# Scaling two projections inside PSUM, and three subtractions per weight tile instead of four, in a hybrid encoder layer

## The chip, the cores and the metric

The kernel runs on one core of one Trainium2 chip. Times are device microseconds of one execution. The core has five engines that run side by side and meet at semaphores: TensorE (PE, matrix products; PEld are its weight loads), VectorE (DVE), ScalarE (ACT), GpSimd (POOL) and SyncE (SP, which here only issues DMAs). Operands lie in SBUF, matrix products land in banks of PSUM. GpSimd works on SBUF tiles alone in this kernel.

## What is computed

One layer of an encoder trunk on 512 tokens of width 1024, in fp32. Cut to what matters here:

```python
h = rmsnorm(x, pre_mix_norm)
z, xbc, dt_raw, q, k, v, gates = split_cols(h @ w_in, IN_SPLITS)
y_ssd = ssd_branch(z, xbc, dt_raw, ...)          # bidirectional scan, 8 groups of 4 heads
y_attn = window_attention(q, k, v, sink, rel_table) @ w_attn_out   # 16 query heads, 4 key heads, width 64
g_ssd, g_attn = split(sigmoid(gates + b_gate))
x = x + rmsnorm((g_ssd * y_ssd + g_attn * y_attn) @ w_o, post_mix_norm)
f = square(relu(rmsnorm(x, pre_mlp_norm) @ w_mlp_in)) @ w_mlp_out
x = x + rmsnorm(f, post_mlp_norm)
```

The change touches the projections that give k (256 columns) and the first part of q, and the preparation of most weight tiles.

## The kernel before, in words

**Products in three parts.** An fp32 product is made of three fast ones. A factor is split into a high part, its rounding to a shorter format (a copy on ScalarE), and a low part, factor minus high part (a subtraction on VectorE or GpSimd). `mm3` (its matmuls are all recorded on the helper line L454) then adds high times high, high times low and low times high into one PSUM bank.

**Weight tiles.** A weight tile is 128 x 1024: eight blocks of 128 columns, one block for each step of a sum over 1024. SP loads it into one of three `wr` buffers. `chunk_split` makes `wh` with one ScalarE copy (L529) and `wl` with GpSimd subtractions (L533): `eng` is `"pppp"`, so four subtractions of 256 columns. Three tiles have 768 columns, so four pieces of 192, and one tile of 768 columns comes with three letters, so three pieces of 256. `wh` and `wl` have three buffers each. The weights of `w_o` and `w_mlp_out` are prepared elsewhere (L1621, L1624), and so are the tiles of the first products (L631, L633).

**Quanta.** The program is a list of quanta. One quantum of `cm` takes one weight tile, runs 24 matmuls (eight blocks, three each, 512 columns) into one bank of the tag `pp`, and calls `done(ps)`, which empties the bank. There are three `pp` banks, taken in turn, and five `ps` banks for everything else. The first quanta are three for v and dt (into `ps`), two for k, two for q with the tokens not yet normalised ("raw"), and then x, q, x, q, B and so on, with the normalised tokens `h`. Between k's first and second quantum the bank `rb` is taken, in which the reciprocal norm of each token is spread over all partitions; ScalarE copies it into the SBUF tile `self.rb` (L738), and eight VectorE operations read the bank to make the normalised tokens (L742).

**After a k quantum** (`k_done`), VectorE multiplies the bank by `self.rb` into the SBUF tile `kf` (L867). From then on the bank is free. Four tiles come of each two heads: for either half of the partitions (a head of width 64) a tile `KH` that holds the head's high part in both halves, and a tile `KL` that holds its low part in both halves. The first is a ScalarE copy from `kf` (L872), the low part a VectorE subtraction from `kf` (L873), and two further copies (L874, L875) bring them to the other half.

**After a raw q quantum** (`done` in `q_quantum`), VectorE scales the bank by 0.125 and by `self.rb` into the SBUF tile `qf` (L898); ScalarE copies a head's high part out of `qf`, blocks of tokens in reverse order (L906), and VectorE subtracts for the low part (L907). The later q quanta do the same straight out of the bank (L911, L912).

**Order.** Every instruction is emitted in program order and then ordered anew by `Planner`: for each engine it plays the program through with costs that are written in the code, gives each instruction a due time that follows from the matmul that needs it, and fixes the order found as each engine's queue. TensorE keeps nearly the program's order. Instructions that use the same PSUM bank are all ordered one after another, whatever they do; instructions that touch the same SBUF columns are ordered if one of them writes. The costs hold a lock between VectorE and GpSimd for some operations. So any edit can move instructions anywhere in the program.

**Slots.** Other SBUF tiles come from 83 slots, handed out in the order in which they were freed; `kf` and `qf` take a slot each for a while.

Of the kernel before, what the change touches and what calls it, by code (L numbers as in the profile page):

```python
# [10 lines left out]
F32 = mybir.dt.float32  # L11
F32R = mybir.dt.float32r
AF = mybir.ActivationFunctionType
ALU = mybir.AluOpType
# [30 lines left out]
FAR, AHEAD = (2,3,5,6,8,9,11,12,), 5  # L45

BACK = 3
WARM = 8
V_CHUNKS = ((0, 2), (2, 5), (5, 8))
W_CHUNKS = ((0, 1), (1, 2), (2, 5), (5, 8))  # L50
# [50 lines left out]
class Slots:  # L101
# [5 lines left out]
    def get(self, name, shape=(128, 512), dtype=F32):  # L107
        s = self.free.popleft()
        self.n += 1
        t = self.pool.tile(list(shape), dtype, tag=f"s{s}", name=f"{name}_{self.n}", bufs=1)  # L110
        self.tags[t.tensor.name] = f"s{s}", 1
        self.slot[id(t)] = (s, t)
        return t
# [279 lines left out]
class Trunk:  # L393
# [117 lines left out]
    def chunk_split(self, i):  # L511
        if len(self.chunks[i]) == 3:
            self.parts[i] = self.chunks[i][1]()
            return
        _, kk, n, eng = self.chunks[i]
        raw = self.raw.pop(i)
        m = kk * n
        hi = self.wp.tile([128, 1024], F32R, tag="wh", name=self.name("wh"), bufs=SPL)
        self.tags[hi.tensor.name] = "wh", SPL
        if eng == "both":  # L520
            view = hi[:, :2 * m].rearrange("p (k u n) -> p k u n", k=kk, u=2)
            r3 = raw.rearrange("p (k n) -> p k n", k=kk)
            self.nc.scalar.copy(view[:, :, 0], r3)
            self.nc.gpsimd.tensor_tensor(view[:, :, 1], r3, view[:, :, 0].bitcast(F32), op=ALU.subtract)
            self.parts[i] = view.rearrange("p k u n -> p k (u n)")
            return
        lo = self.wp.tile([128, 1024], F32R, tag="wl", name=self.name("wl"), bufs=SPL)
        self.tags[lo.tensor.name] = "wl", SPL
        self.nc.scalar.copy(hi[:, :m], raw)  # L529
        engines = {"v": self.nc.vector, "p": self.nc.gpsimd}  # L530
        for e, c in zip(eng, range(0, m, m // len(eng))):
            c = slice(c, c + m // len(eng))
            engines[e].tensor_tensor(lo[:, c], raw[:, c], hi[:, c].bitcast(F32), op=ALU.subtract)  # L533
        v = lambda t: t[:, :m].rearrange("p (k n) -> p k n", k=kk)
        self.parts[i] = (v(hi), v(lo))

# [127 lines left out]
    def start(self):  # L664
# [13 lines left out]
        pg = self.bank("pp")  # L678
        for _ in range(WARM):
            self.mm(pg[:, :128], ones, ones, True, True)  # L680
# [179 lines left out]
    def kv_quanta(self):  # L860
        nc = self.nc
        get = self.slots.get
        self.KH, self.KL = [], []

        def k_done(ps):
            x = get("kf")
            nc.vector.tensor_tensor(x, ps, self.rb, op=ALU.mult)  # L867
            for j in range(2):
                a = slice(j * 64, j * 64 + 64)
                b = slice(64 - j * 64, 128 - j * 64)  # L870
                KH, KL = get("KH", dtype=F32R), get("KL", dtype=F32R)
                nc.scalar.copy(KH[a], x[a])  # L872
                nc.vector.tensor_tensor(KL[a], x[a], KH[a].bitcast(F32), op=ALU.subtract)  # L873
                nc.scalar.copy(KH[b], x[a])  # L874
                nc.scalar.copy(KL[b], KL[a])  # L875
                self.KH.append(KH)
                self.KL.append(KL)
            self.slots.put(x)

        hh = lambda: self.hr  # L880
        return [self.cm(self.d_w_in_b, C_K - 64 + 128 * i, hh, k_done) for i in range(2)]
# [5 lines left out]
    def q_quantum(self, i):  # L887

        nc = self.nc

        blocks = lambda ap: ap.rearrange("p (n t) -> p n t", t=128)

        raw = i < RAW_Q

        def done(ps):
            if raw:
                x = self.slots.get("qf")
                nc.vector.scalar_tensor_tensor(x, ps, 0.125, self.rb, op0=ALU.mult, op1=ALU.mult)  # L898
            for u in range(2):
                a = slice(u * 64, u * 64 + 64)  # L900
                b = slice(64 - u * 64, 128 - u * 64)
                q = self.slots.get("Q", dtype=F32R)
                if raw:
                    self.Q[2 * i + u] = q
                    back = self.backward(x[a])
                    nc.scalar.copy(blocks(q[a]), back)  # L906
                    nc.vector.tensor_tensor(blocks(q[b]), back, blocks(q[a]).bitcast(F32), op=ALU.subtract)  # L907
                    continue
                self.Q[2 * i + u] = q
                back = self.backward(ps[a])  # L910
                nc.scalar.activation(blocks(q[a]), back, AF.Copy, scale=0.125)  # L911
                nc.vector.scalar_tensor_tensor(blocks(q[b]), back, 0.125, blocks(q[a]).bitcast(F32), op0=ALU.mult, op1=ALU.subtract)  # L912

            if raw:
                self.slots.put(x)
            if i == RAW_Q - 1:
                self.slots.put(self.rb, *sum(self.hr, ()))

        return self.cm(self.d_w_in_b, C_Q - 64 + 128 * i, lambda: self.hr if raw else self.h, done)

    def attn_bias(self, h):
# [643 lines left out]
    def folded_quanta(self, part):  # L1565
# [95 lines left out]
        if last:  # L1661
            if part == 3:
                self.at(len(self.quanta) + BACK, self.load_x1)
            for name, lead in MIX_LEAD if part == "o" else (('B11', 4), ('B22', 4), ('B12', 4), ('B21', 3)):
# [122 lines left out]
```

## Time and profile before

| | us |
|---|---|
| median of 3 runs | 1072.91 |
| lowest, highest | 1072.71, 1074.02 |
| the profiled execution | 1075.79 |
| span of its profile, first to last instruction | 1074.0 |
| TensorE busy in the span | 1060.2 (99%) |
| GpSimd busy | 796.0 (74%) |
| VectorE busy | 771.8 (72%) |
| ScalarE busy | 658.4 (61%) |
| mean granted TensorE clock | 0.998 of full speed |

The profiled execution took 2.88 us more than the median and 1.8 us more than its own span. A row of a group names line, engine, operation, what it writes and reads, its shape and count, then busy time and mean duration, then the idle time of the engine before such instructions and what ended it. A row of the timeline has its start and length in us, and in brackets the idle time before it. Neighbouring instructions of one engine overlap a little in the record, and the ends of matmuls are modelled, so the step from start to start says more on TensorE than the length.

### The profile page before, as it was taken

To read this page: it belongs to the slowest core of one execution; us is meant where nothing else is said; L and a number is where in the kernel's file an instruction comes from. 1 tells how busy PE (TensorE), PEld (TensorE's weight loads), DVE (VectorE), ACT (ScalarE), POOL (GpSimd) and SP (SyncE) were. 2 spreads that over 40 slices of the span, in tenths; PEclk is the share of its full clock that TensorE was granted. 3 is DMA by queue.
4 is the path that set the end of the run, shared out by engine and by line. 5 is a ranking of instruction groups with operands and counts; after the bars stand their busy time and mean duration, and the time that the engine had idled before them with its cause. 6 is when DMAs were issued, how large, how long until landed. Compare 5 with 4: busy or idle time off the path is not lost.

```text
span 1074.0 us, 16639 instructions
## 1 busy us (share of the span) xinstructions
PE 1060.2 (99%) x5542; PEld 893.8 (83%) x5542; DVE 771.8 (72%) x1354; ACT 658.4 (61%) x1409; POOL 796.0 (74%) x991
## 2 busy tenths in 40 slices
PE   9999999999999999999999999999999999999997
PEld 8878888888888888888888788889888888888885
DVE  6986877797795868787877626698663574574588
ACT  7875786676686857676777424466555444444552
POOL 4856557557668798999989956215587898898994
PEclk9999999999999999999999999999999999999999
DMA  8443333433434535255535444317221421434232
GB/s 316 140 128 101 102 102 111 130 102 116 123 99 128 163 102 171 88 142 148 170 92 157 159 147 148 111 59 263 89 69 65 153 98 60 157 96 141 78 99 78
DMA packets 62085, 134.25 MB, mean 125 GB/s; under 512 B 9128, under 2 KB 18984, under 8 KB 62000
## 3 DMA queue, kind: packets, MB, share of 16 engines
q1 hardware_dynamic: 61712, 132.96, 38.4%
q8 instruction: 43, 0.70, 0.3%
q14 instruction: 42, 0.34, 0.1%
q10 hardware_dynamic: 288, 0.23, 0.1%
HBM read 128.68 MB, written 4.49 MB: 124 GB/s over the span
## 4 chain that ended last, share of the span: by engine, by line
PE 86%; DVE 7%; POOL 2%; issue 2%; DMA 2%; ACT 1%; DVEq 0%; SPq 0%; POOLq 0%; ACTq 0%
PE pp L454 54%; PE ps L454 30%; PE ps L458 2%; DMA x<-in_x 1%; POOL wl L533 1%; DVE yl L1321 1%; POOL w L1222 1%; DVE P L941 1%; DVE u L1017 1%; DVE xt L742 0%; DVE P L955 0%; DMA xt<-in_xt 0%; DVE h L745 0%; DVE dtw L816 0%; DVE u L1024 0%
## 5 line engine op out<-in xcount | busy, mean ns | idle before, releaser
L533 POOL TENSOR_TENSOR wl<-wr,wh 128x256 fp32r<-128x256 f32 (+1 forms) x519 | 415.4, 830 | 180.7 <-ACT wh L529 172.7
L454 PE MATMUL pp<-h,wh 128*128 128x512 f32 (+1 forms) x1664 | 504.6, 385 | 0.0
L454 PEld LDWEIGHTS pp<-h,wh 128*128 128x128 f32 x1664 | 306.3, 188 | 59.2 <-issue 0.5
L454 PE MATMUL pp<-h,wl 128*128 128x512 f32 (+1 forms) x832 | 321.3, 386 | 0.0
L529 ACT CAST wh<-wr 128x1024 fp32r<-128x1024 f32 (+1 forms) x130 | 135.1, 1041 | 122.8 <-PE pp L454 97.8
L454 PEld LDWEIGHTS pp<-h,wl 128*128 128x128 f32 x832 | 156.4, 188 | 30.9 <-POOL wl L533 0.2
L1624 POOL TENSOR_TENSOR wl<-wd,wh 128x256 fp32r<-128x256 f32 x158 | 131.7, 871 | 11.8 <-ACT wh L1621 11.8
L1621 ACT CAST wh<-wd 128x512 fp32r<-128x512 f32 x92 | 53.2, 618 | 38.3 <-PE ps L454 21.6
L454 PE MATMUL ps<-wl,fh 128*128 128x512 f32 x184 | 71.7, 390 | 0.0
L454 PE MATMUL ps<-wh,fh 128*128 128x512 f32 x184 | 71.6, 389 | 0.0
L454 PE MATMUL ps<-wh,fl 128*128 128x512 f32 x184 | 71.6, 389 | 0.0
L1459 DVE SCALAR_TENSOR_TENSOR pp<-pp,r 128x256 f32<-128x256 f32 (+1 forms) x31 | 17.3, 559 | 64.8 <-ACT r L1456 64.7
L1183 ACT ACTIVATE n<-cb,tables 128x128 f32<-128x128 f32 x128 | 47.7, 393 | 15.5 <-DVE cb L1174 13.6
L1017 DVE SCALAR_TENSOR_TENSOR u<-pp,cv,u 128x510 f32<-128x510 f32 (+1 forms) x64 | 47.8, 746 | 8.6 <-ACT u L1013 7.2
L1184 ACT ACTIVATE m<-cb,tables 128x128 f32<-128x128 f32 x128 | 47.6, 390 | 7.2 <-DVE cb L1174 6.4
L1222 POOL TENSOR_TENSOR w<-w,E 128x256 f32<-128x256 f32 x48 | 40.5, 858 | 10.7 <-DVE w L1218 9.8
L1179 ACT ACTIVATE rf<-rf,tables 128x128 f32<-128x128 f32 x128 | 42.1, 393 | 2.9 <-DMA rf<-csT 2.8
L1185 DVE TENSOR_TENSOR m<-m,n 128x512 f32<-128x512 f32 x32 | 30.1, 942 | 17.4 <-ACT m L1184 17.0
L1676 DVE TENSOR_TENSOR acc<-acc,ps 128x512 f32<-128x512 f32 x46 | 31.3, 681 | 15.6 <-PE ps L454 15.5
L1177 POOL TENSOR_TENSOR rb<-rb,tables 128x512 f32<-128x512 f32 x32 | 36.7, 1149 | 6.2 <-DMA rb<-csT 4.7
L1115 POOL TENSOR_TENSOR xd<-x,tables 128x256 f32<-128x256 f32 x48 | 34.1, 730 | 9.4 <-ACT th L1023 2.5
L454 PEld LDWEIGHTS ps<-wl,fh 128*128 128x128 f32 x184 | 34.5, 188 | 7.5 <-POOL wl L1624 0.3
(289 smaller groups left out, 2266.9 us busy)
## 6 DMA issues: line engine op xcount, KB each, us to landing
wr<-in_w_in_b SPq DMA_DIRECT2D x74, 512.0 KB, 3.5
wr<-in_w_mlp_in_b SPq DMA_DIRECT2D x32, 512.0 KB, 3.5
wd<-in_w_mlp_out SPq DMA_DIRECT2D x64, 256.0 KB, 5.6
rb<-csT SPq DMA_DIRECT2D x32, 256.0 KB, 3.8
rf<-csT SPq DMA_DIRECT2D x32, 256.0 KB, 3.6
wr<-in_w_ssd_out_b SPq DMA_DIRECT2D x13, 512.0 KB, 3.8
x<-in_x SPq DMA_DIRECT2D x16, 256.0 KB, 4.5
E<-csE SPq DMA_DIRECT2D x32, 128.0 KB, 4.3
```

The costliest lines, as they stand in the source:

```text
L454: self.nc.tensor.matmul(out, lhsT, rhs, start=start, stop=stop, skip_group_check=more)
L529: self.nc.scalar.copy(hi[:, :m], raw)
L533: engines[e].tensor_tensor(lo[:, c], raw[:, c], hi[:, c].bitcast(F32), op=ALU.subtract)
L1017: nc.vector.scalar_tensor_tensor(u[:, a:e], ps[:, a + d:e + d], self.wtap(t, b), u[:, a:e], op0=ALU.mult, op1=ALU.add)
L1115: nc.gpsimd.tensor_tensor(v4(xd[:, d * 256:(d + 1) * 256]), v4(xs(c)), by_dir(self.coef, c)[:, d].unsqueeze(2).to_broadcast([128, 4, 64]), ...
L1177: nc.gpsimd.tensor_tensor(v4(rb), v4(rb), cs[:, 1].unsqueeze(2).to_broadcast([128, 4, 128]), op=ALU.subtract)
L1179: nc.scalar.activation(v4(rf)[:, h], v4(rf)[:, h], AF.Identity, bias=ncs[:, 0, h:h + 1])
L1183: nc.scalar.activation(v4(n)[:, h], cb[:, 0], AF.Copy, scale=dt[:, 0, h:h + 1])
L1184: nc.scalar.activation(v4(m)[:, h], cb[:, 1], AF.Copy, scale=dt[:, 1, h:h + 1])
L1222: nc.gpsimd.tensor_tensor(wc, wc, E[:, d], op=ALU.add)
L1621: nc.scalar.copy(hi, src)
L1624: (nc.vector if q == 512 else nc.gpsimd).tensor_tensor(lo[:, c], src[:, c], hi[:, c].bitcast(F32), op=ALU.subtract)
```

## The change

1. The constant `PIECES = 3` is added. In `chunk_split` the low part is cut into three pieces whatever `eng` says, and all go to GpSimd. For 1024 columns the cuts are 341 and 682; the second piece starts one column early, so the pieces are columns 0 to 340, 340 to 681 and 682 to 1023, and column 340 is written twice with the same value. For 768 columns the pieces are 0 to 255, 255 to 511 and 512 to 767.
2. `k_done` multiplies inside the PSUM bank instead of into `kf`. One ScalarE copy and one VectorE subtraction over all 128 partitions make the high and low parts of both heads in the tiles of index 0. Then halves are copied: the second head's parts into both halves of tile 1, and the first head's parts over the second's in tile 0. The high parts are copied from the bank, the low parts from `L[0]`.
3. The raw q quanta scale inside the PSUM bank instead of into `qf`, and copy and subtract from the bank.

```diff
 BACK = 3
+PIECES = 3
 WARM = 8
...
         self.nc.scalar.copy(hi[:, :m], raw)
-        engines = {"v": self.nc.vector, "p": self.nc.gpsimd}
-        for e, c in zip(eng, range(0, m, m // len(eng))):
-            c = slice(c, c + m // len(eng))
-            engines[e].tensor_tensor(lo[:, c], raw[:, c], hi[:, c].bitcast(F32), op=ALU.subtract)
+        cuts = [m * j // PIECES for j in range(PIECES + 1)]
+        for j, (a, b) in enumerate(zip(cuts, cuts[1:])):
+            c = slice(a - (j==1), b)
+            self.nc.gpsimd.tensor_tensor(lo[:, c], raw[:, c], hi[:, c].bitcast(F32), op=ALU.subtract)
...
         def k_done(ps):
-            x = get("kf")
-            nc.vector.tensor_tensor(x, ps, self.rb, op=ALU.mult)
-            for j in range(2):
-                a = slice(j * 64, j * 64 + 64)
-                b = slice(64 - j * 64, 128 - j * 64)
-                KH, KL = get("KH", dtype=F32R), get("KL", dtype=F32R)
-                nc.scalar.copy(KH[a], x[a])
-                nc.vector.tensor_tensor(KL[a], x[a], KH[a].bitcast(F32), op=ALU.subtract)
-                nc.scalar.copy(KH[b], x[a])
-                nc.scalar.copy(KL[b], KL[a])
-                self.KH.append(KH)
-                self.KL.append(KL)
-            self.slots.put(x)
+            nc.vector.tensor_tensor(ps, ps, self.rb, op=ALU.mult)
+            H, L = ([get(n, dtype=F32R) for _ in range(2)] for n in ("KH", "KL"))
+            a, b = slice(0, 64), slice(64, 128)
+            nc.scalar.copy(H[0], ps)
+            nc.vector.tensor_tensor(L[0], ps, H[0].bitcast(F32), op=ALU.subtract)
+            for c in (b, a):
+                nc.scalar.copy(H[1][c], ps[b])
+                nc.scalar.copy(L[1][c], L[0][b])
+            nc.scalar.copy(H[0][b], ps[a])
+            nc.scalar.copy(L[0][b], L[0][a])
+            self.KH += H
+            self.KL += L
...
         def done(ps):
             if raw:
-                x = self.slots.get("qf")
-                nc.vector.scalar_tensor_tensor(x, ps, 0.125, self.rb, op0=ALU.mult, op1=ALU.mult)
+                nc.vector.scalar_tensor_tensor(ps, ps, 0.125, self.rb, op0=ALU.mult, op1=ALU.mult)
...
                 if raw:
                     self.Q[2 * i + u] = q
-                    back = self.backward(x[a])
+                    back = self.backward(ps[a])
                     nc.scalar.copy(blocks(q[a]), back)
                     nc.vector.tensor_tensor(blocks(q[b]), back, blocks(q[a]).bitcast(F32), op=ALU.subtract)
                     continue
...
-            if raw:
-                self.slots.put(x)
             if i == RAW_Q - 1:
                 self.slots.put(self.rb, *sum(self.hr, ()))
```

## The prediction

> **What bounds the kernel now.** I read the page first, then TensorE's waits, then the chain that ended last.
>
> ```profile
> span 1074.0 us, 16639 instructions
> PE 1060.2 (99%) x5542; PEld 893.8 (83%) x5542; DVE 771.8 (72%) x1354; ACT 658.4 (61%) x1409; POOL 796.0 (74%) x991
> PEclk9999999999999999999999999999999999999999
> ```
>
> ```profile
> 82.28 9.78 PE pp L454 x43
> ```
>
> ```profile
> PE pp L454 <- DVE yl L1321: 2.6, 1, 2.6
> PE ps L454 <- ACT pT L966: 1.6, 1, 1.6
> PE pp L454 <- DVE two L673: 1.0, 1, 1.0
> PE ps L458 <- DVE P L955: 0.4, 2, 0.2
> PE ps L454 <- DVE hr L480: 0.2, 1, 0.2
> ```
>
> TensorE is the bound. The second fence, a row of the chain, gives 43 matmuls in 9.78 us, 0.227 us each, back to back; no edit here removes a matmul. The third is all that TensorE waits for in the whole span: 5.8 us, of which 4.2 us are two events. So the most that this change can win is about 4 us (0.4%), and it can lose wherever it makes a third event. A difference under 0.2% (2.1 us) is about what a measurement of this kernel can't tell from none.
>
> The first event lies at the end of a stretch in which VectorE, not TensorE, leads the chain. The rows of the chain and then two stretches of busy time:
>
> ```profile
> 57.11 0.69 DVE Q L907
> 57.81 0.69 DVE KL L873
> 59.22 0.49 DVE KL L873
> 60.56 0.69 DVE KL L873
> ...
> 74.79 0.38 ACT pT L966
> 75.21 1.20 PE ps L454 x6
> ```
>
> ```profile
> 27.00:50.00 23.00, 23.00 (x107) 19.26 (x106) 21.34 (x39) 18.21 (x34) 22.19 (x28) 1.00 0.44 140
> 50.00:75.00 25.00, 23.57 (x120) 19.80 (x118) 22.89 (x48) 19.84 (x43) 11.97 (x16) 1.00 0.44 137
> ```
>
> The third busy figure is VectorE: 21.34 of 23 us and 22.89 of 25 us. The four subtractions of K and those of Q lie in this queue, and the chain runs through them until 75.21 us, where TensorE has stood for 1.6 us.
>
> **Part 1, three pieces.** What a piece costs, alone:
>
> ```profile
> 53.48 2.83 POOL L533 TENSOR_TENSOR wl<-wr,wh 128x256 fp32r<-128x256 f32 x4 [3.79 <-ACT wh L529]
> ```
>
> ```profile
> 614.47 2.24 POOL L533 TENSOR_TENSOR wl<-wr,wh 128x192 fp32r<-128x192 f32 x4
> ...
> 627.15 0.20 POOL L447 TENSOR_SCALAR rcol<-rcol 128x4 f32<-128x4 f32 x1
> 627.43 1.02 POOL L449 TENSOR_TENSOR rcol<-rcol,mhalf 128x4 f32<-128x4 f32 x1
> ```
>
> Four pieces of 256 take 2.83 us, four of 192 take 2.24: 0.59 us for 256 columns, 2.3 ns a column, which leaves 0.12 us fixed a piece. Three pieces with 1026 columns are 3 x 0.12 + 2.36 = 2.72 us, 0.11 less a tile. Against that stands the shared column: the second piece writes what the first wrote. The trace has no such pair on GpSimd; the nearest is L447 and L449, where the second needs the first and starts 0.08 us after its end, while pieces now overlap by some 0.05. If the shared column makes it wait likewise, a tile costs 2.72 + 0.13 = 2.85 us. So between -0.11 and +0.02 us for each of some 126 tiles: -14 to +3 us of GpSimd time. I take the wait, so nothing. Does either end reach TensorE?
>
> ```profile
> POOL wl L533 <- ACT wh L529: 172.7, 66, 36.4
> ACT wh L529 <- PE pp L454: 97.8, 38, 5.8
> ```
>
> ```profile
>   PEld pp L454: 0.2, 1
> ```
>
> GpSimd stands for 172.7 us until ScalarE has copied, and that copy waits for TensorE to give back a buffer; in the list of those that waited for these subtractions, TensorE's weight loads have 0.2 us in all. The first block of a tile is ready 0.2 us later (341 columns instead of 256), hidden by tiles made two quanta ahead. Price on the path: 0. Without that cover it would be 0.2 us a tile. The three-piece tile of 768 columns keeps its length, and three of four pieces change likewise.
>
> **Part 2, K and Q in PSUM.** The rows of the old tiles and the nearest ones for the new forms:
>
> ```profile
> L873 DVE TENSOR_TENSOR KL<-kf,KH x4: 677/683/689, 34.1 to 60.6; 64x512 fp32r<-64x512 f32 x4
> L867 DVE TENSOR_TENSOR kf<-pp,rb x2: 683/683/683, 26.9 to 37.8; 128x512 f32<-128x512 f32 x2
> ```
>
> ```profile
> L907 DVE TENSOR_TENSOR Q<-qf,Q x4: 687/785/1115, 39.9 to 61.3; 64x512 fp32r<-64x512 f32 x4
> L898 DVE SCALAR_TENSOR_TENSOR qf<-pp,rb x2: 681/682/683, 38.4 to 49.0; 128x512 f32<-128x512 f32 x2
> ```
>
> ```profile
> L872 ACT CAST KH<-kf x4: 617/620/622, 27.7 to 40.3; 64x512 fp32r<-64x512 f32 x4
> ...
> 59.06 0.59 ACT L911 ACTIVATE Q<-pp 64x512 fp32r<-64x512 f32 x1
> ...
> 59.85 0.68 DVE L912 SCALAR_TENSOR_TENSOR Q<-pp,Q 64x512 fp32r<-64x512 f32 x1
> ...
> L1676 DVE TENSOR_TENSOR acc<-acc,ps 128x512 f32<-128x512 f32 x46 | 31.3, 681 | 15.6 <-PE ps L454 15.5
> ```
>
> VectorE: four subtractions of 0.68 become two, over all partitions and out of PSUM, 0.68 each (L1676): -1.4 us. The four of Q, 0.69 to 1.12, become 0.68 (L912, the same shape out of a bank): about -0.6, since two of them stood behind GpSimd. The scalings stay at 0.68. Together -2.0 us. ScalarE: twelve copies of 0.62 for K become fourteen, eight of them out of PSUM at 0.59: +1.0 us; Q's four -0.1.
>
> What is hidden before and may not be now: the banks. A bank was free after one scaling; now it is held until the last copy out of it, and all its users go in turn. K's first bank (scaled from 26.95 us) is the one that q's first quantum takes.
>
> ```profile
> 26.95 0.68 DVE L867 TENSOR_TENSOR kf<-pp,rb 128x512 f32<-128x512 f32 x1
> ...
> 29.48 1.05 ACT L529 CAST wh<-wr 128x1024 fp32r<-128x1024 f32 x1
> ```
>
> ```profile
> 37.24 0.61 PE L454 MATMUL pp<-hr,wh 128*128 128x512 f32 x2
> ...
> 49.56 0.62 PE L454 MATMUL pp<-h,wh 128*128 128x512 f32 x2
> ```
>
> The second q quantum starts at 37.24, so the first at 37.24 - 24 x 0.227 = 31.8 us. Scaling, copy, subtraction, three copies: 0.68 + 0.59 + 0.68 + 3 x 0.59 = 3.7 us, from 26.95 to 30.7: 1.1 us to spare. The weight copy of 1.05 us on ScalarE fits in between; one more copy of 0.62 would cost TensorE 0.6. So 0 to 0.6; I take 0. For the later banks, K's second subtraction and the first quantum's second Q subtraction, now due before 49.56 us instead of at 57 to 60, put 1.4 us into a VectorE queue that is full there: 0 to 1.4 us for TensorE, by what the queue can't push back. I take 0, since the displaced work (maxima of the first head) is due later and ScalarE's idle time before 36 us leaves VectorE a gap.
>
> The event at 75 us: VectorE arrives 2.0 us sooner at the copies for which TensorE stood 1.6 us. Between 0 (the slips above eat it) and -1.6; I take -1.6, the row nearest being VectorE's own saving.
>
> **Part 3, the other event.** Nothing in the diff names it, but its cause is GpSimd's pieces:
>
> ```profile
> 610.61 6.65 DVE L1321 TENSOR_TENSOR yl<-yT,yh 128x512 fp32r<-128x512 f32 x1 [6.02 <-ACT yh L1320]
> ```
>
> ```profile
> 611.12 5.59 POOL L533 TENSOR_TENSOR wl<-wr,wh 128x192 fp32r<-128x192 f32 x9
> ```
>
> One subtraction on VectorE ran for 6.65 us, until nine GpSimd pieces in a row were through; TensorE paid 2.6 us. Both read two SBUF operands, and VectorE lost every hand-over. The Trainium skill ("SBUF — State Buffer", Who interferes with whom) says that whichever starts first holds the shared pair for its whole instruction and the other blocks until then. By that rule the block would end with one piece and no such event could come; the rows show nine pieces, so the measurement decides here, and I keep the event as a risk. In the changed kernel the 0.08 us gap inside each tile, if it is there, would let VectorE in after at most three pieces. Whether the timed runs hold this event I can only bound: the profiled execution stands 2.88 us above the median, about its 2.6, which suggests that the timed runs mostly go without it.
>
> **Sum.** Against the profiled execution: 1075.79 - 1.6 = 1074.2, and 1071.6 with the second event gone. Against the median, which I take to be without it: 1072.91 + 0 - 1.6 = **1071.3 us**. Work moved by the planner elsewhere I set at 0: after 76 us TensorE waits for nothing else over 0.4 us, so its orders mostly come out covered. The diff issues no DMA, and the loads of weights keep their buffers; the four slots that `kf` and `qf` no longer take shift which slot later tiles get, which the same sentence covers.
>
> **The rivals.**
> 1. Both events go. If the timed runs do hold the block, and the gap or the shifted times break it: 1072.91 - 1.6 - 2.6 = 1068.7. For it: one such event in the whole trace, hence easily undone. Against it: the 2.88 us.
> 2. Nothing moves: the saving on VectorE is eaten by the held banks (0.6 + 1.4 = 2.0), and three pieces with a wait take as long as four, so the change doesn't do what it says: 1072.9.
> 3. Slower: a VectorE subtraction is blocked behind a run of GpSimd pieces where it wasn't before, in the stage from 400 to 640 us where GpSimd is fullest. Price of one as in the trace: 2.6 us on TensorE, and with the gain lost 1072.91 + 2.6 = 1075.5. It decides when the block outlasts TensorE's cover there, 6.65 - 2.6 = 4 us, which is five pieces of 0.9 us in a row. For it: pieces grow, so every block grows by a quarter. Against: only one in the old trace.
>
> **How the numbers follow.** Chances: my forecast 0.34, of which a third lies beyond 0.2% (the wait measured from start to start is nearer 1.9); rival 1 0.25; rival 2 0.13; rival 3, which also stands for any other new wait by moved work, 0.28. Faster by over 0.2%: 0.25 + 0.12 = 0.37. Slower: 0.28. Within: 0.35. The likeliest one's own range is 1070.7 to 1072.9 (from -1.9 with a little to spare, to 0). The range over all, down to rival 1 with 1 us more from small waits and up to rival 3, is 1067.7 to 1075.9.
>
> **What would show it.** Right: three subtractions of about 0.95 us on L533 for each tile; two K subtractions instead of four; no wait of TensorE near 73 us; no VectorE instruction over 2 us beside reciprocals. Wrong: TensorE waiting at 32 or 44 to 50 us for a `pp` bank; a gap over 0.2 us between pieces one and two; a VectorE subtraction of several us beside a run of L533; or pieces from an odd column (the tiles of 768) that run longer than 0.74 us.

## The result and the profile after

| | before | after |
|---|---|---|
| median of 15 runs, us | 1073.36 | 1071.20 |
| lowest to highest | 1072.61 to 1075.17 | 1070.61 to 1072.07 |
| the profiled execution | 1075.79 | 1071.39 |
| its span | 1074.0 | 1069.4 |

The ratio is 0.9978, with a 95% interval of 0.9972 to 0.9985: faster by 0.22%. The lines of the changed kernel are numbered one higher than the old ones up to `k_done`, and three lower behind `q_quantum`. Its page and all that TensorE waits for:

```profile
span 1069.4 us, 16514 instructions
PE 1059.7 (99%) x5542; PEld 894.1 (84%) x5542; DVE 774.7 (72%) x1352; ACT 658.4 (62%) x1411; POOL 770.3 (72%) x862
```

```profile
PE pp L455 <- DVE two L674: 1.0, 1, 1.0
PE ps L459 <- DVE P L952: 0.5, 1, 0.5
```

Of the 5.8 us of waits 1.5 are left. Both large ones are gone, and a new one of 0.5 us (near 55 us, the first head's probabilities) has come. That is -4.3 of the -4.6 us between the two spans. The timed runs differ by 2.16 only, since the old profiled execution lay 2.4 us above its median and the new one at it.

The changed parts in the timeline and by tile: one weight tile's three pieces on GpSimd, K's subtractions, Q's, and two stretches of busy time.

```profile
54.66 2.81 POOL L534 TENSOR_TENSOR wl<-wr,wh 128x341 fp32r<-128x341 f32 x3 [5.24 <-ACT wh L530]
```

```profile
L871 DVE TENSOR_TENSOR KL<-pp,KH x2: 683/688/692, 28.6 to 41.2; 128x512 fp32r<-128x512 f32 x2
```

```profile
L905 ACT CAST Q<-pp x4: 582/583/586, 39.3 to 52.3; 64x512 fp32r<-64x512 f32 x4
L906 DVE TENSOR_TENSOR Q<-pp,Q x4: 685/691/694, 40.1 to 53.7; 64x512 fp32r<-64x512 f32 x4
```

```profile
27.00:50.00 23.00, 23.00 (x108) 19.31 (x107) 22.46 (x38) 20.18 (x36) 20.36 (x23) 1.00 0.38 132
50.00:75.00 25.00, 24.38 (x124) 20.39 (x123) 21.61 (x50) 19.67 (x45) 11.73 (x13) 1.00 0.41 137
```

A tile takes 2.81 us instead of 2.83. K has two subtractions of 0.69 us instead of four, and Q's no longer vary: none stands behind GpSimd. In the two stretches the fourth busy figure from PE on, ScalarE's, is up by 2.0 and down by 0.2 us; the last busy figure, GpSimd's, is 20.36 us in the first stretch, against 22.19 before. The third, VectorE's, is up by 1.1 and down by 1.3 us: over both stretches it has hardly changed (44.07 against 44.23), but K's and Q's subtractions come earlier. The last ones start at 41.2 and 53.7 us, before at 60.6 and 61.3.

And where the old profile had the block of 6.65 us, VectorE and GpSimd in the new one:

```profile
607.78 0.69 DVE L1318 TENSOR_TENSOR yl<-yT,yh 128x512 fp32r<-128x512 f32 x1 [6.16 <-ACT yh L1317]
```

```profile
607.84 6.65 POOL L534 TENSOR_TENSOR wl<-wr,wh 128x256 fp32r<-128x256 f32 x7
```

The same subtraction meets a run of seven pieces again and takes 0.69 us: it started 0.06 us ahead of the run, not behind it.

### The profile page after: what moved, and what is told of

Its sections match the earlier page's. It is cut to its first block, busy times and chain, and to the rows that moved or that the text cites. A ratio compares the mean times of both kernels' runs of the same rounds, so it can differ in the third digit from the quotient of the medians.

```text
span 1069.4 us, 16514 instructions
## 1 busy us (share of the span) xinstructions
PE 1059.7 (99%) x5542; PEld 894.1 (84%) x5542; DVE 774.7 (72%) x1352; ACT 658.4 (62%) x1411; POOL 770.3 (72%) x862
## 4 chain that ended last, share of the span: by engine, by line
PE 90%; DVE 5%; DMA 2%; ACT 2%; issue 1%; POOL 0%; DVEq 0%; POOLq 0%; ACTq 0%
PE pp L455 57%; PE ps L455 30%; PE ps L459 3%; DMA row<-in_row 1%; DMA x<-in_x 1%; DVE P L952 1%; DVE u L1014 1%; DMA xt<-in_xt 0%; DVE h L746 0%; POOL wl L1621 0%; DMA wr<-in_wv 0%; ACT P L946 0%; DVE dtw L817 0%; DVE Q L911 0%; DVE x L1416 0%
## 5 line engine op out<-in xcount | busy, mean ns | idle before, releaser
L534 POOL TENSOR_TENSOR wl<-wr,wh 128x342 fp32r<-128x342 f32 (+2 forms) x390 | 385.7, 1004 | 209.5 <-ACT wh L530 200.8
L455 PEld LDWEIGHTS ps<-wh,fh 128*128 128x128 f32 x184 | 34.5, 188 | 7.2
L455 PEld LDWEIGHTS ps<-wh,fl 128*128 128x128 f32 x184 | 34.5, 188 | 7.0
```

Of the source, the lines that this page charges most:

```text
L455: self.nc.tensor.matmul(out, lhsT, rhs, start=start, stop=stop, skip_group_check=more)
L534: self.nc.gpsimd.tensor_tensor(lo[:, c], raw[:, c], hi[:, c].bitcast(F32), op=ALU.subtract)
```

## The experiments

Theory A is that of the prediction: VectorE's time before 75 us pays, the pieces are hidden. Theory B: the pieces pay. Theory C: the planner's new orders decide.

**The two parts alone.** The pieces with K and Q as before:

```diff
 k_done, q_quantum: as before
 chunk_split: three pieces, the second one column early, as in the change
```

> The three pieces with the shared column, K and Q as before. Theory A (the gain comes from K and Q in PSUM, the pieces are hidden): within 0.5 us of the kernel before, TensorE's 1.6 us wait near 73 us still there, the block of yl behind L533 near 610 us gone or shorter than three pieces. Theory B (the gain comes from GpSimd's shorter load and the gap inside each tile): 1.5 to 2.2 us faster than before. Theory C (moved orders and slots decide, any edit gives its own number): anything from 2 us faster to 2 us slower, and not the same sum as the two parts give together.

Measured: 1072.32 us median against 1073.37, ratio 0.9990 (0.9981 to 0.9999). TensorE's waits:

```profile
PE pp L455 <- DVE two L674: 1.0, 1, 1.0
PE ps L455 <- ACT pT L967: 1.0, 1, 1.0
```

That is a gain of 1.05 us where theory A had 0. Its interval reaches from 0.1 to 2.0 us, but the wait near 73 us is also down, to 1.0, with K and Q untouched; the four profiles with the old K and Q and four pieces have 1.4 to 2.2 us there. So theory A fails on this part by the median, though the interval doesn't exclude a gain of under 0.5 us.

K and Q alone:

```diff
 k_done, q_quantum: in PSUM, as in the change
 chunk_split: four pieces of 256, as before
```

> K and Q in PSUM, four pieces of 256 as before. Theory A: 1.3 to 2.2 us faster than before, no TensorE wait over 1 us between 60 and 80 us, and the changed kernel is within 0.5 us of this one. Theory B: within 0.5 us of before. Theory C: no sum rule with the pieces alone.

Measured: 1071.80 against 1073.37, ratio 0.9984 (0.9975 to 0.9993), so 1.57 us faster. The wait near 73 us is gone:

```profile
PE pp L455 <- DVE two L674: 1.0, 1, 1.0
PE ps L459 <- DVE P L952: 0.4, 2, 0.2
```

The two parts give 1.05 and 1.57 us alone, 2.62 in sum, and 2.16 together. Both take from the same wait near 73 us, so they needn't add up. What the pieces add to K and Q is 0.6 us by the medians, inside the intervals, and no wait shows it: the waits in TensorE's list come to 1.4 us with K and Q alone and to 1.5 with both.

**K and Q apart.** K alone, then Q alone, four pieces in both:

```diff
 k_done: in PSUM        # K alone
 q_quantum: by way of qf
```

> K in PSUM alone; Q by way of qf, four pieces. Theory A by its terms: VectorE saves 1.4 us before 62 us, so TensorE's wait near 73 us shrinks from 1.6 to about 0.2, and the kernel is 0.8 to 1.6 us faster than before. If the held banks cost more than they save, TensorE waits at 32 or at 44 us and the gain is under 0.5.

```diff
 k_done: by way of kf   # Q alone
 q_quantum: in PSUM
```

> Q in PSUM alone; K by way of kf, four pieces. Theory A by its terms: VectorE saves 0.6 us, so 0.3 to 0.8 us faster than before and the wait near 73 us about 1 us. If orders decide (theory C), there is no relation between the VectorE time saved and the gain, and K alone and Q alone do not add up to both.

Measured, each against 1073.34: K alone 1071.70, ratio 0.9981 (0.9972 to 0.9990); Q alone 1072.85, ratio 0.9987 (0.9979 to 0.9996). By the medians that is 1.64 and 0.49 us. The waits, K alone first:

```profile
PE pp L454 <- DVE two L673: 1.0, 1, 1.0
PE ps L458 <- DVE P L954: 0.4, 2, 0.2
PE ps L454 <- ACT pT L965: 0.3, 1, 0.3
```

```profile
PE ps L459 <- DVE P L953: 1.2, 3, 0.8
PE pp L455 <- DVE two L674: 1.0, 1, 1.0
PE ps L455 <- ACT pT L964: 0.3, 1, 0.3
```

K saves 1.4 us of VectorE and gains 1.6, Q saves 0.6 and gains 0.5. Q alone removes most of the wait at 73 us too, but TensorE then waits 0.8 us near 55 us for the first head's probabilities (P), which stand on VectorE behind the Q work that now comes earlier. The other 0.4 us for P are two waits of 0.2 near 98 and 227 us, which K alone and the kernel before have as well. K and Q together (1.57) gain no more than K alone.

**VectorE's time given back.** The changed kernel with K's low parts in four subtractions over half the partitions, out of the same bank:

```diff
-            nc.vector.tensor_tensor(L[0], ps, H[0].bitcast(F32), op=ALU.subtract)
+            for c in (a, b):
+                nc.vector.tensor_tensor(L[0][c], ps[c], H[0][c].bitcast(F32), op=ALU.subtract)
```

> The changed kernel with K's two subtractions over 128 partitions made as four over 64 each, out of the same bank: VectorE gets back 1.4 us before 62 us, nothing else changes in kind. Theory A: 0.5 to 1.4 us slower than the changed kernel, with TensorE's wait near 73 us back in part. Rival (the gain comes of K's bank use, of freed slots or of the pieces, not of VectorE's time): within 0.3 us of the changed kernel.

Measured: 1072.51 against 1071.20 for the changed kernel; ratio to before 0.9988 (0.9979 to 0.9996). So 1.3 us slower than the change, as theory A wanted, though the two medians come from different runs of the kernel before (1073.34 and 1073.36). A wait came elsewhere than forecast, at 44 us, ahead of the products of `dtw`:

```profile
PE ps L455 <- DVE dtw L821: 1.1, 1, 1.1
PE pp L455 <- DVE two L674: 1.0, 1, 1.0
```

```profile
42.28 0.69 DVE L872 TENSOR_TENSOR KL<-pp,KH 64x512 fp32r<-64x512 f32 x1
...
43.93 1.18 DVE L821 SCALAR_TENSOR_TENSOR dtw<-tables,row 128x256 f32<-128x256 f32 x1
```

And `dtw` in the changed kernel:

```profile
42.69 1.07 DVE L821 SCALAR_TENSOR_TENSOR dtw<-tables,row 128x256 f32<-128x256 f32 x1
```

VectorE's queue had a fourth K subtraction 1.6 us ahead of `dtw`, which starts 1.2 us later than in the changed kernel. VectorE's time ahead of 44 us is on the path of the changed kernel: shown. What took away the wait near 73 us is not settled by this run, as that wait stayed away: it can be less work on VectorE, or K's and Q's subtractions coming earlier.

**The block.** The kernel before, once more:

> The kernel before, unchanged, for a second profile. If the 6.65 us block of yl near 610 us is an accident of single executions, this profile may be without it, its span is then some 2.6 us shorter (1071.4 instead of 1074.0), and the timed runs fall into two groups 2 to 2.6 us apart. If it comes in every execution, it is there again and the span is 1074.

Measured: 1073.11 against 1073.34, ratio 0.9997 (0.9985 to 1.0009). The profile holds no such block, and the wait near 73 us is 2.0 instead of 1.6:

```profile
PE ps L454 <- ACT pT L966: 2.0, 1, 2.0
PE pp L454 <- DVE two L673: 1.0, 1, 1.0
```

So the block is an accident of single executions. The span was 1073.1, not the 1071.4 expected, and this execution (1074.93) also lay above its median. The difference of 1.7 us is TensorE's clock. The wait ends at 75.84 us, and 1.5 us later the granted clock (the figure behind the five busy figures) is at half for 3.4 us, which costs 1.7:

```profile
75.84 0.45 PE L454 MATMUL ps<-KH,Q 128*128 128x384 f32 x1 [2.03 <-ACT pT L966]
```

```profile
77.30:80.70 3.40, 3.40 (x10) 2.63 (x9) 2.22 (x10) 1.89 (x7) 0.37 (x1) 0.50 0.48 157
```

In this stretch matmuls start 0.43 us apart instead of 0.23. The first profile of the kernel before, with 1.6 us here, has no such stretch. Two clean groups of times 2.6 us apart did not show: of 33 runs of the kernel before beside the first experiments, 21 lie from 1072.5 to 1073.7 and 12 spread from 1074.0 to 1076.2. Ten of these 12 have a mean granted clock of 0.996 or 0.997, of the 21 only four; that fits a stretch at half clock in some executions, but single runs have no trace, so it isn't shown.

**The shared column.** The changed kernel without it:

```diff
-            c = slice(a - (j==1), b)
+            c = slice(a, b)
```

> The changed kernel without the shared column: pieces 0 to 340, 341 to 681, 682 to 1023, so the second starts at an odd column and waits for nothing of the first. Theory A: the 0.08 us gap after the first piece becomes an overlap of 0.04, a tile takes 2.69 us instead of 2.81, GpSimd loses about 15 us of occupied time, and the time stays within 0.5 us of the changed kernel. If an odd start column costs something, the second piece runs longer than 0.93 us; I expect 0.93, as the pieces of 257 columns from column 255 ran at 0.74. Theory B: 1 us or more away from the changed kernel.

Measured: 1071.54, ratio 0.9980 (0.9971 to 0.9989). A tile is shorter, as forecast, and an odd first column costs nothing:

```profile
54.50 2.69 POOL L534 TENSOR_TENSOR wl<-wr,wh 128x341 fp32r<-128x341 f32 x3 [3.45 <-ACT wh L530]
```

Within 0.5 us of the change: here the pieces are hidden. Its profile shows two things that the prediction had spoken of: TensorE waiting at 32 us for K's bank, and a block.

```profile
PE pp L455 <- ACT KH L875: 0.8, 1, 0.8
```

```profile
1012.83 6.09 DVE L473 TENSOR_TENSOR fl<-fs,fh 128x512 fp32r<-128x512 f32 x1 [0.38 <-ACT fh L472]
```

TensorE's list has no wait for this block: what it costs depends on what is due next.

The pieces alone without the column:

```diff
 pieces_alone, with c = slice(a, b)
```

> The pieces alone without the shared column: 341, 341 and 342 columns, no gap. If the gain of the pieces alone is GpSimd's load, this keeps it or adds to it (1.0 to 1.5 us faster than before). If it is the gap, this is within 0.4 us of before, and blocks of 3 us and more on VectorE show up in the profile or as slow single executions. If it is the order found, anything else.

Measured: 1074.04 median of 12, ratio 0.9994 (0.9982 to 1.0005), but no run lies between 1071.7 and 1073.9: five are from 1070.8 to 1071.6, seven from 1074.0 to 1075.6. The profiled one is of the upper group, and this is what is in it, VectorE, GpSimd and TensorE:

```profile
35.16 5.98 DVE L874 TENSOR_TENSOR KL<-kf,KH 64x512 fp32r<-64x512 f32 x1
```

```profile
35.98 0.95 POOL L534 TENSOR_TENSOR wl<-wr,wh 128x341 fp32r<-128x341 f32 x1
36.86 1.46 POOL L746 TENSOR_TENSOR h<-xt,h 128x256 fp32r<-128x256 f32 x2
...
39.11 1.48 POOL L746 TENSOR_TENSOR h<-xt,h 128x256 fp32r<-128x256 f32 x2
```

```profile
44.99 0.39 PE L455 MATMUL ps<-KH,Q 128*128 128x256 f32 x1 [2.05 <-DVE Q L908]
```

One K subtraction stood behind a gapless run of GpSimd pieces for 5.3 us more than its 0.69, and Q, due later on VectorE, came 2 us late for TensorE. That is the mechanism of rival 3, in the old form of K. It cost more than the wait, as half clock followed at once:

```profile
45.60:49.00 3.40, 3.40 (x12) 2.87 (x11) 3.33 (x9) 1.77 (x4) 0.98 (x2) 0.50 0.03 9
```

The wait and 1.7 us for the clock make 3.7 us; the medians of the two groups are 3.4 apart. Blocks over 2 us stood in three of the eight profiles of kernels without the shared column, and in none of the six with it.

Four pieces with the shared column, and the same instructions as before in another order:

```diff
-            c = slice(c, c + m // len(eng))
+            c = slice(c - (c == m // len(eng)), c + m // len(eng))
```

> The kernel before with four pieces, of which the second starts one column early (256, 257, 256, 256 columns), so it waits 0.08 us for the first; nothing else is changed. The pieces alone came out about 1.05 us faster by the medians, which my theory had at 0. If that gain is the gap (VectorE gets in, blocks end), it comes here too: 0.7 to 1.3 us faster than before, and no VectorE instruction over 2 us. If it is GpSimd's load or the number of pieces, this is 0 to 0.5 us slower than before, as a tile takes 2.95 us instead of 2.83. If it is the order that the planner finds, this kernel has its own wait near 73 us, neither that of before nor that of the pieces.

```diff
 Planner.depend: the second piece of each tile is ordered after the first
 (an edge for the planner alone; the instructions are those of before)
```

> The kernel before with every instruction the same, but the planner is told that the second of a tile's four pieces must follow the first, so it charges the wait of 0.08 us and finds another order for all engines; the chip itself waits for nothing. If orders decide what the piece edits are worth (theory C), this differs from before by more than 0.5 us, to either side, and has TensorE waits of its own near 73 us or 560 us. If orders are worth little, it is within 0.4 us of before, and the 1.05 us of the pieces alone and the 3 us that four pieces with a shared column lose come from the pieces on the chip.

Measured: four pieces with the column 1076.44 against 1073.66, ratio 1.0029 (1.0017 to 1.0040); the other order alone 1073.16 against 1073.43, ratio 0.9997 (0.9985 to 1.0009). TensorE's waits in the first of the two, then in the second:

```profile
PE ps L454 <- ACT pT L966: 2.2, 1, 2.2
PE ps L454 <- ACT sh L471: 2.1, 1, 2.1
PE pp L454 <- DVE two L673: 1.0, 1, 1.0
```

```profile
PE ps L454 <- ACT pT L966: 1.4, 1, 1.4
PE pp L454 <- DVE two L673: 1.0, 1, 1.0
PE ps L458 <- DVE P L955: 0.4, 2, 0.2
```

The loss of 2.8 us is one event. The 3000th matmul starts at 526.6 us (527.2 in the kernel before), the 3300th at 586.3 (583.2). Between them lie the wait for `sh`, near 562 us, and half clock from about its end on:

```profile
561.80:565.10 3.30, 3.21 (x9) 2.63 (x10) 2.35 (x4) 2.59 (x7) 3.22 (x4) 0.50 0.20 63
```

So the gap alone brought no gain, but the median says little of what it does elsewhere. The product of `sh` stands two matmuls later in TensorE's order than in the kernel before; whether this order or the longer tile made `sh` late isn't shown. The one other order tried is worth nothing that can be measured. It isn't the same order as that of the four pieces with the column, so an order's worth is bounded by one sample only.

**Fewer, longer pieces.** The changed kernel with two:

```diff
-PIECES = 3
+PIECES = 2
```

> The changed kernel with two pieces of 512 and 513 columns, the second one column early. By the fixed 0.12 us a piece the tile takes about 2.7 us alone, pieces of 1.32 us. Theory A: within 0.7 us of the changed kernel, since TensorE has tiles two quanta ahead. The rival that longer pieces block VectorE longer: VectorE instructions with two SBUF inputs take on average 0.1 to 0.2 us more, and TensorE waits add 1 us or more, most in the stage from 200 to 640 us.

Measured: 1074.91 against 1073.37, ratio 1.0010 (1.0001 to 1.0019): 3.7 us slower than three pieces, though a tile takes 2.68 us instead of 2.81. The waits, then the VectorE instruction behind the second of them and GpSimd's tile:

```profile
PE ps L455 <- ACT sh L472: 1.3, 1, 1.3
PE ps L459 <- DVE u L1021: 1.2, 1, 1.2
```

```profile
527.03 1.75 DVE L1021 SCALAR_TENSOR_TENSOR u<-th,u 128x512 f32<-128x512 f32 x1 [0.24 <-ACT th L1020]
```

```profile
122.74 2.68 POOL L534 TENSOR_TENSOR wl<-wr,wh 128x512 fp32r<-128x512 f32 x2 [4.12 <-ACT wh L530]
```

VectorE's `u` took 1.75 us for some 0.7 of work, and TensorE stood for it. It isn't alone: 32 VectorE instructions of this profile took 1.6 to 1.8 us; in the others none did, reciprocals and the three blocks left out. The longer piece blocks longer, in the stage where rival 3 put it. That explains the second wait. The first, 1.3 us near 561 us, is for the product that four pieces with the column waited for too, and it stands at the same place in TensorE's order, so an order may be its cause.

**K and the pieces, Q as before.**

```diff
 k_done: in PSUM; chunk_split: three pieces with the shared column
 q_quantum: by way of qf
```

> K in PSUM and the three pieces with the shared column, Q by way of qf as before. K alone had gained as much as K and Q together, so Q may add nothing: then this is within 0.3 us of the changed kernel. If VectorE's time still counts there, this is 0.3 to 0.6 us slower than the changed kernel.

Measured: 1070.86 (nine runs), ratio 0.9977 (0.9967 to 0.9986), the same as the change's 0.9978 within the intervals. Q's part adds nothing to the other two.

## Why the prediction was right, and where it was not

The forecast was 1071.3 us, the measured median 1071.20. The time is right; the sum behind it is right in its main term and too small in another, and its base was too low.

**K and Q in PSUM, -1.6.** Right in size: 1.57 us alone, with the wait of 1.6 us gone. The terms hold one by one: the subtractions 0.69 us each, the copies out of PSUM 0.58 to 0.59, Q's free of GpSimd. Giving VectorE its time back cost 1.3 us (for the 1.4 of the sum). That K saves 1.4 and Q 0.6 was right as VectorE time; as TensorE time K alone takes it all. The step from 2.0 us of VectorE time to a wait of 1.6 gone is in part argued: that the subtractions now come earlier may do as much, and no run has the time saved with all of them at their old places.

**The held banks, 0.** Right in the change, with less room than the 1.1 us worked out. The copies of K's first bank end just before ScalarE's next weight copy:

```profile
30.51 0.58 ACT L875 CAST KH<-pp 64x512 fp32r<-64x512 f32 x1
31.11 1.05 ACT L530 CAST wh<-wr 128x1024 fp32r<-128x1024 f32 x1
```

That is 0.7 us ahead of 31.8, and without the shared column the 0.8 us wait appeared there.

**The pieces, 0.** The tile's length was right (2.81 for 2.85), and so was the wait of the second piece. But the step "Price on the path: 0" failed by the median of the pieces alone. It asked only whether TensorE waits for `wl`. It passed over the last busy figure of the row from 27 to 50 us, which was in the prediction: GpSimd 22.19 of 23 us, as full as VectorE, and the block of 6.65 us had shown that VectorE can stand behind GpSimd. Alone, the pieces gained 1.05 us, and GpSimd's busy time in that stretch went down:

```profile
27.00:50.00 23.00, 23.00 (x108) 19.27 (x107) 21.72 (x39) 17.92 (x32) 20.89 (x23) 1.00 0.43 139
```

That this time is the cause isn't shown. With the old K and Q the shortest tile (2.69 us) has the lowest group of runs, 1070.8 to 1071.6, then come 2.81 us with 1072.32 and 2.83 with 1073.4; the 1076.44 of the longest tile tells nothing of this stretch, since its loss lies near 562 us. Each of these kernels also has its own order, and order alone was tried once. In the sum a tile has 1025 columns, not 1026, which changes nothing.

**The second event, 0 against the median.** The inference from the 2.88 us was right in kind: the second profile of before was without the block. In the changed kernel it is gone as well. The base was a little low: three runs gave 1072.91, fifteen 1073.36. With the pieces at 0 the forecast from 1073.36 would have been 1071.8, which is what K and Q alone gave (1071.80). By the medians the pieces made up the other 0.6, with the reservation made above. That the forecast met the median to 0.1 us is luck: a base too low and a gain left out cancelled each other.

**The rivals.** Rival 1 (1068.7) did not come: as far as the two profiles of before tell, the median execution held no block to lose. Rival 2 is out, as K's and Q's saving arrived whole. Rival 3 did not come for the change, but its mechanism is real: two pieces met it in the stage from 400 to 640 us. Its point of decision, five pieces in a row, was not what decided; a single block of 1.1 us was enough where a product was due.

## What to carry to other kernels

Where a kernel is bound by TensorE, look for the one or two waits it has left and ask which engine leads the chain before each; time saved there is worth up to the wait, whatever the number of edits, and here 1.7 us more where half clock followed the wait. Read every engine's busy time in that stretch, not only that of the engine the edit relieves. Where VectorE and GpSimd both read two SBUF operands, moving one of VectorE's into PSUM freed it here from GpSimd's pieces (Q's subtractions: 0.69 to 1.12 us before, 0.69 after), and a gapless run of GpSimd work is a risk to whatever VectorE has next.

## What was unexpected of the hardware

- A VectorE instruction with two SBUF operands can wait for a whole run of GpSimd instructions, not for one: 6.65, 5.98 and 6.09 us for work of 0.69, in three profiles of eight, and not in each execution of the same kernel (it was there in one of two profiles of the kernel before). The Trainium skill ("SBUF — State Buffer", Who interferes with whom) has the loser wait for the instruction that holds the lock; these rows differ from it.
- A dependent second piece on GpSimd starts 0.08 us after the first instead of 0.04 before its end. None of the six profiles with this gap inside the tiles holds a block over 1.2 us; but five of the eight without it hold none either, so that the gap is the reason isn't shown.
- TensorE ran 3.4 us at a granted clock of 0.50 after three waits of 2.0 to 2.1 us, in three of the fourteen profiles (the last 6 us of each left out). Two longer waits, of 2.6 us in the first profile of the kernel before and of 2.2 us near 73 us in four pieces with the column, had none behind them. What decides isn't shown.
